# Float32 value product on two halves of the array, and a stick-breaking product moved to GpSimd

## The chip, the cores and the metric

The kernel runs on one core of a Trainium2 chip. Its engines are TensorE (PE, with weight loads as PEld), VectorE (DVE), ScalarE (ACT), GpSimd (POOL) and SyncE (SP, which issues the DMAs). The metric is the device time of one execution in microseconds, lower is better.

## The reference

One layer of a hybrid encoder block on 2048 tokens of 1024 channels: RMSNorm, one input projection, a Mamba-2 SSD branch, a stick-breaking attention branch with 16 heads of 64 channels, a gated merge, an output projection, RMSNorm and the residual. The change lies in the attention branch:

```
logits = einsum('bqhd,bkhd->bhqk', q[:, q0:kend], k[:, :kend]) * scale
mask = ki < qi
log_fail = where(mask, log_sigmoid(-logits), 0)
between = cumsum(log_fail, reverse) - log_fail
w = where(mask, exp(log_sigmoid(logits) + between), 0)
out = einsum('bhqk,bkhd->bqhd', w, v[:, :kend])
```

The kernel takes the sum of logarithms as a running product: t = sigmoid(-logits) is multiplied from the newest key to the oldest, and w = sigmoid(logits) times the running product of the keys behind.

## The kernel before

Everything that is projected from the input goes through `product`: weights and activations are each split in a high and a low fp32r part, and three fp32r products of 512 columns stand for one float32 product. The projections of v go to DRAM (`vst`) with both parts beside each other, 64 + 64 columns a head; k and q lie in `kst` and `qst`, split in the same way. After the SSD stage (whose state output `yp` is made by float32 products with 64 columns of weights) follows the attention loop over `steps`: a step is (head h, 512 queries qs, 512 keys kc), 160 in all, keys from the diagonal block (kc = qs) backward. Of the ten steps of a head four are diagonal and six are full.

A step works on four query blocks of 128 (i) and four key blocks of 128 (kb). `attn_qk(s + 1, i)` makes the logits `lg` of query block i in the next step by two fp32r products, two sigmoids on ScalarE (t in tile `tc`, w in tile `sw`), on diagonal steps two affine selects on GpSimd (L847, L849), the running product as a scan on VectorE (L852), and the product of w and the running product on VectorE (L853). GpSimd copies the scan's last column (`cy`, L856) as the start of the next step's scan, and sets one column of `tc` to 1. `attn_tr(s, kb)` transposes the weights of key block kb on TensorE: one transposition for each query block, all into one tile `wtp`; `attn_tr(s, 0)` reads all four `sw` tiles of the step. ScalarE and VectorE split the result in `wh` and `wl` (L870, L872), and `attn_av` multiplies both with v into `po`.

All products and transpositions are chained on TensorE in the order in which the code writes them (`chain`). Into the gaps `fill(i)` puts products of projections that are needed later: 3264 of them over the first 150 steps, spread over the places of a step by the weights FW, and with them the evictions, stores and weight preparation that belong to them. The last head's ten steps are filled with the first products of the next stage (`fill_y`), prepared by `first_y`, which also puts sums on GpSimd (L695).

Of the kernel before, what the change touches and what calls it, by code (L numbers as in the profile page):

```python
# [23 lines left out]
HD = 64  # L24
EPS = 1e-6
WARM = 24
FW = (0.8, 0.9, 1.0, 1.0, 1.1, 1.2)

COL_Z = 0
COL_X = 1024  # L30
# [18 lines left out]
def hybrid_kernel(ctx, tc, x, norm_pre, w_in, b_gate, conv_w, conv_b, dt_bias, a_log, d_skip,  # L49
# [57 lines left out]

    kst = [drp.tile([P, L], F32, name=f"kst{h}") for h in range(HEADS)]
    qst = [drp.tile([P, L], F32, name=f"qst{h}") for h in range(HEADS)]
    vst = [drp.tile([L, 4, P], F32, name=f"vst{i}") for i in range(HEADS // 4)]  # L110
    csd = drp.tile([HEADS, L], F32, name="csd")
    ytd = [drp.tile([D, TB], F32, name=f"ytd{t}") for t in range(NTB)]
    otd = [drp.tile([D, TB], F32, name=f"otd{t}") for t in range(NTB)]
# [272 lines left out]
    with tc.tile_pool(name="va", bufs=2) as va, tc.tile_pool(name="vp", bufs=2, space=PSUM) as vp:  # L386
# [16 lines left out]
        def unit_v(i, c, wv):  # L403
            c0, cw = vch[i]
            vh, vl = wv
            off = cw - VW
            tb, o = c // CPB, (c % CPB) * P
            ps = vp.tile([P, TB], F32, name="vps", tag="vps", bufs=3)
            for k in range(KT):
                xh, xl = hh[tb][:, k, o:o + P], hl[tb][:, k, o:o + P]  # L410
                matmul(ps[:, :cw], xh, vh[k], start=(k == 0), stop=False)
                yield
                matmul(ps[:, :cw], xh, vl[k], start=False, stop=False)
                yield
                matmul(ps[:, :cw], xl, vh[k], start=False, stop=(k == KT - 1))
                yield
            if off:
                nc.vector.tensor_copy(kn[:, c, :], ps[:, :16])
            v = va.tile([P, 4, 2, HD], F32R, name="vt", tag="vt", bufs=3)
            src = ps[:, off:cw].rearrange("p (h d) -> p h d", d=HD)  # L420
            nc.scalar.copy(v[:, :, 0, :], src)
            nc.vector.tensor_sub(v[:, :, 1, :], src, v[:, :, 0, :].bitcast(F32))
            nc.sync.dma_start(vst[i][c * P:(c + 1) * P], v.bitcast(F32).rearrange("p h s d -> p h (s d)"))

        def last_k():
            knf = kn.rearrange("p c d -> p (c d)")
# [352 lines left out]

    steps = [(h, qs, kc) for h in range(HEADS) for qs in reversed(range(NTB)) for kc in reversed(range(qs + 1))]  # L780
    last_head = min(i for i, s in enumerate(steps) if s[0] == HEADS - 1)
    fills = {"gen": fill_h(), "left": n_main, "pos": 6 * last_head, "acc": 0.0, "late": False}

    def tick():
        clock[0] += 1
# [3 lines left out]
    def fill(i):  # L789
        f = fills  # L790
        if f["pos"] <= 0:
            for _ in f["gen"]:
                tick()
            if f["late"]:
                return
            f.update(gen=fill_y(box_y), left=8 * 24, pos=6 * (len(steps) - last_head) - 3, acc=0.0, late=True)
        f["acc"] += f["left"] / f["pos"] * FW[i]
        f["pos"] -= 1
        while f["acc"] >= 1.0:
            f["acc"] -= 1.0  # L800
            f["left"] -= 1
            if next(f["gen"], 0) == 0:
                f["left"] = 0
                break
            tick()
# [3 lines left out]
    def attn_load(s):  # L809
# [11 lines left out]
        if (h, kc) not in kts:  # L821
            k = ab.tile([P, TB], F32R, name="kt", tag="kt", bufs=4)
            nc.sync.dma_start(k.bitcast(F32), kst[h][:, kc * TB:(kc + 1) * TB])
            v = ab.tile([P, CPB, P], F32R, name="vt", tag="vt", bufs=4)
            nc.sync.dma_start(v.bitcast(F32), vst[h // 4][kc * TB:(kc + 1) * TB, h % 4, :].rearrange(
                "(c p) d -> p c d", p=P))
            kts[h, kc], vts[h, kc] = k, v

    def attn_qk(s, i):
# [20 lines left out]
                                    pattern=[[-1, P]], channel_multiplier=1)  # L850
        tr = t[:, W::-1]
        nc.vector.tensor_tensor_scan(tr, tr, tr, 1.0 if diag else carry[h, qs, i], ALU.mult, ALU.min)  # L852
        nc.vector.tensor_mul(w[:, :W], w[:, :W], t[:, 1:W + 1])  # L853
        if kc > 0:
            c = ab.tile([P, 1], F32, name="cy", tag="cy", bufs=8)
            nc.gpsimd.tensor_copy(c, t[:, 0:1])  # L856
# [5 lines left out]
    def attn_tr(s, kb):  # L862
        h, qs, kc = steps[s]
        q0 = kb if kc == qs else 0
        lo = q0 * P
        tp = ap.tile([P, TB], F32, name="wtp", tag="wtp", bufs=3)
        for i in range(q0, CPB):
            transpose(tp[:, i * P:(i + 1) * P], ws[s, i][:, kb * P:(kb + 1) * P], ident)
        wh = ab.tile([P, TB], F32R, name="wh", tag="wh", bufs=3)
        nc.scalar.copy(wh[:, lo:], tp[:, lo:])  # L870
        wl = ab.tile([P, TB], F32R, name="wl", tag="wl", bufs=3)
        nc.vector.tensor_sub(wl[:, lo:], tp[:, lo:], wh[:, lo:].bitcast(F32))  # L872
        wts[s, kb] = lo, wh, wl

    def attn_av(s, kb):
        h, qs, kc = steps[s]
        lo, wh, wl = wts.pop((s, kb))
        if (h, qs) not in pos:
            pos[h, qs] = ap.tile([P, TB], F32, name="po", tag="po", bufs=1)
        po, v = pos[h, qs], vts[h, kc]  # L880
        first = kc == qs and kb == 0
        final = kc == 0 and kb == CPB - 1
        matmul(po[:, lo:], v[:, kb, :], wh[:, lo:], start=first, stop=False, skip_group_check=True)
        matmul(po[:, lo:], v[:, kb, :], wl[:, lo:], start=False, stop=final, skip_group_check=True)
        if final:
            e0 = (h % 2) * HD
            mine, other = slice(e0, e0 + HD), slice(HD - e0, P - e0)
            z = ab.tile([P, TB], F32, name="zl", tag="zl", bufs=1)
# [15 lines left out]
    for s in range(len(steps)):  # L904
        attn_load(s + 2)
        for i in range(CPB):
            attn_tr(s, i)
            attn_qk(s + 1, i)
            if i >= 2:
                attn_av(s, i - 2)  # L910
            fill(i)
        for i in range(2, CPB):
            attn_av(s, i)
            fill(i + 2)
    for _ in fills["gen"]:
        pass
    close_ap()
# [150 lines left out]
```

## Time and profile before

| | |
|---|---|
| median of 3 runs (lowest, highest) | 3164.92 us (3163.69, 3165.49) |
| span of the profiled execution | 3163.6 us |
| TensorE products, busy | 3024.1 us (96%) |
| TensorE weight loads, busy | 2496.9 us (79%) |
| VectorE, busy | 2457.2 us (78%) |
| ScalarE, busy | 1585.7 us (50%) |
| GpSimd, busy | 477.9 us (15%) |
| mean granted TensorE clock | 0.993 |

The span is that of one profiled execution, from its first to its last instruction; durations in the text come from it. A record of a product on TensorE is longer than the time until the next one starts, since products overlap in the array; so TensorE's busy share says little of how full it is, and the starts are what counts. The attention loop takes the time from 936 us to about 2663 us.

### The profile page before, as it was taken

How to read it: one execution, taken by the hardware profiler on the slowest of the kernel's cores; microseconds unless marked ns; L12 is line 12 of the kernel's file. 1: busy time of each engine (PE TensorE's matmuls, PEld its weight loads, DVE VectorE, ACT ScalarE, POOL GpSimd, SP SyncE). 2: the span in 40 equal slices, each digit the busy share in tenths (PEclk: the TensorE clock that was granted, in tenths of full speed). 3: DMA queues.
4: the chain of work that ended last, by engine and by line, in shares of the span. 5: the costliest groups of instructions: out<-in, count | busy, mean ns of one | idle time of the engine just before them, and what ended most of it. 6: DMA issues, size and time to landing. Idle time of an engine off the chain costs nothing.

```text
span 3163.6 us, 48155 instructions
## 1 busy us (share of the span) xinstructions
PE 3024.1 (96%) x16169; PEld 2496.9 (79%) x16169; DVE 2457.2 (78%) x4357; ACT 1585.7 (50%) x3102; POOL 477.9 (15%) x1626
## 2 busy tenths in 40 slices
PE   8999999999999999999999999999999989999998
PEld 6899888787877777777777777777777767888887
DVE  7321688768869989989899999989998899756553
ACT  6211345434446666566565666566665656333321
POOL 0000011100111212122212121222111231101000
PEclk9999999999999999999999999999999999999999
DMA  5532022212243334224323333334233334555452
GB/s 165 148 122 93 24 71 80 68 40 67 72 128 89 90 89 110 80 81 113 93 70 103 94 97 91 87 94 114 69 89 90 111 117 144 176 148 167 133 167 70
DMA packets 298816, 320.63 MB, mean 101 GB/s; under 512 B 23148, under 2 KB 187848, under 8 KB 298568
## 3 DMA queue, kind: packets, MB, share of 16 engines
q1 hardware_dynamic: 298416, 317.51, 34.6%
q8 instruction: 128, 2.10, 0.3%
q14 instruction: 120, 0.98, 0.1%
q10 hardware_dynamic: 152, 0.05, 0.0%
HBM read 216.67 MB, written 100.79 MB: 100 GB/s over the span
## 4 chain that ended last, share of the span: by engine, by line
PE 53%; DVE 33%; issue 5%; DMA 4%; ACT 4%; POOL 1%; SPq 0%; DVEq 0%; POOLq 0%; ACTq 0%
PE proj L74 30%; DVE tc L852 13%; PE po L74 8%; DVE sw L853 7%; PE vps L74 6%; DVE wl L872 5%; PE wtp L77 4%; PE lg L74 3%; DMA csb<-csd 2%; ACT sw L845 1%; ACT wh L870 1%; PE yp L74 1%; DVE acc L474 1%; DVE o L893 1%; DVE o L892 1%
## 5 line engine op out<-in xcount | busy, mean ns | idle before, releaser
L74 PE MATMUL proj<-hh,whi 128*128 128x512 f32 x1920 | 762.0, 397 | 0.1
L74 PE MATMUL proj<-hh,wlo 128*128 128x512 f32 x1920 | 761.7, 397 | 0.0
L74 PE MATMUL proj<-hl,whi 128*128 128x512 f32 x1920 | 760.4, 396 | 1.3 <-DVE hl L286 1.1
L870 ACT CAST wh<-wtp 128x512 fp32r<-128x512 f32 (+3 forms) x640 | 337.1, 527 | 390.2 <-PE wtp L77 386.6
L852 DVE TENSOR_TENSOR_SCAN tc<-tc,cy 128x513 f32<-128x513 f32 x384 | 490.9, 1278 | 0.3 <-ACT tc L843 0.3
L872 DVE TENSOR_TENSOR wl<-wtp,wh 128x512 fp32r<-128x512 f32 (+3 forms) x640 | 383.0, 599 | 81.5 <-ACT wh L870 80.3
L77 PE MATMUL wtp<-ident,sw 128*128 128x128 f32 x2176 | 369.9, 277 | 72.2 <-DVE sw L853 70.1
L853 DVE TENSOR_TENSOR sw<-sw,tc 128x512 f32<-128x512 f32 (+3 forms) x640 | 394.2, 616 | 50.5 <-POOL sw L849 13.5
L77 PEld LDWEIGHTS wtp<-ident,sw 128*128 128x128 f32 x2176 | 280.7, 141 | 181.0 <-DVE sw L853 99.1
L74 PEld LDWEIGHTS proj<-hl,whi 128*128 128x128 f32 x1920 | 362.6, 189 | 72.6 <-DVE hl L286 2.5
L74 PEld LDWEIGHTS proj<-hh,wlo 128*128 128x128 f32 x1920 | 362.6, 189 | 70.7 <-issue 0.3
L74 PEld LDWEIGHTS proj<-hh,whi 128*128 128x128 f32 x1920 | 362.7, 189 | 70.1 <-ACT hh L285 0.5
L845 ACT ACTIVATE sw<-lg 128x512 f32<-128x512 f32 (+3 forms) x640 | 346.1, 541 | 49.8 <-PE wtp L77 49.6
L843 ACT ACTIVATE tc<-lg 128x512 f32<-128x512 f32 (+3 forms) x640 | 349.1, 545 | 18.7 <-PE lg L74 13.1
L132 ACT CAST whi<-wraw 128x512 fp32r<-128x512 f32 x248 | 154.3, 624 | 280.5 <-PE proj L74 178.9
L74 PE MATMUL lg<-kt,qa 128*128 128x512 f32 (+3 forms) x640 | 285.1, 445 | 0.0
L74 PE MATMUL po<-wl,vt 128*128 128x512 f32 (+3 forms) x640 | 242.6, 379 | 29.0 <-DVE wl L872 28.2
L852 DVE TENSOR_TENSOR_SCAN tc<-tc 128x129 f32<-128x129 f32 (+3 forms) x256 | 218.1, 852 | 26.3 <-POOL tc L847 25.2
L74 PE MATMUL lg<-kt,qb 128*128 128x512 f32 (+3 forms) x640 | 234.6, 367 | 0.0
L74 PE MATMUL po<-wh,vt 128*128 128x512 f32 (+3 forms) x640 | 232.4, 363 | 0.0
L134 DVE TENSOR_TENSOR wlo<-wraw,whi 128x512 fp32r<-128x512 f32 x246 | 173.4, 706 | 73.3 <-ACT whi L132 70.5
L856 POOL COPY cy<-tc 128x1 f32<-128x1 f32 x384 | 133.6, 348 | 448.7 <-DVE tc L852 448.7
(202 smaller groups left out, 4887.8 us busy)
## 6 DMA issues: line engine op xcount, KB each, us to landing
wraw<-in_w_in SPq DMA_DIRECT2D x120, 256.0 KB, 3.0
vst<-vt SPq DMA_DIRECT2D x64, 256.0 KB, 2.0
csb<-csd SPq DMA_DIRECT2D x64, 256.0 KB, 4.4
qa<-qst SPq DMA_DIRECT2D x64, 256.0 KB, 3.5
qb<-qst SPq DMA_DIRECT2D x128, 128.0 KB, 3.8
kt<-kst SPq DMA_DIRECT2D x64, 256.0 KB, 3.2
vt<-vst SPq DMA_DIRECT2D x64, 256.0 KB, 3.0
gtd<-zb SPq DMA_DIRECT2D x64, 256.0 KB, 2.1
```

What stands on the lines that cost most here:

```text
L74: chain(nc.tensor.matmul(*a, **k))
L77: chain(nc.tensor.transpose(*a))
L132: nc.scalar.copy(h, raw)
L134: (eng or nc.vector).tensor_tensor(l, raw, h.bitcast(F32), op=ALU.subtract)
L474: nc.vector.scalar_tensor_tensor(acc, xp[:, i:i + TB], pv[:, col:col + 1], acc, op0=ALU.mult, op1=ALU.add)
L843: nc.scalar.activation(t[:, :W], lg[:, :W], AF.Sigmoid, scale=-0.125)
L845: nc.scalar.activation(w[:, :W], lg[:, :W], AF.Sigmoid, scale=0.125)
L852: nc.vector.tensor_tensor_scan(tr, tr, tr, 1.0 if diag else carry[h, qs, i], ALU.mult, ALU.min)
L853: nc.vector.tensor_mul(w[:, :W], w[:, :W], t[:, 1:W + 1])
L856: nc.gpsimd.tensor_copy(c, t[:, 0:1])
L870: nc.scalar.copy(wh[:, lo:], tp[:, lo:])
L872: nc.vector.tensor_sub(wl[:, lo:], tp[:, lo:], wh[:, lo:].bitcast(F32))
```

## The change

The value product becomes one float32 product for each key block: v is stored and loaded as it is, without a split, the transposed weights are copied once (`wt`), and the 64 columns of v stand as weights on the lower or the upper half of the array, by the parity of the key block. Each half sums its own two key blocks in its half of `po`; the two halves are added at the end as before. On diagonal steps key block 1 is widened to all 512 columns, with zeros. All four value products of step s - 1 are now issued in step s, after its second query block. The fill has five places a step in place of six. The product of stick weight and running product moves from VectorE to GpSimd.

```diff
--- before.py
+++ after.py
@@ -24,7 +24,7 @@
 HD = 64
 EPS = 1e-6
 WARM = 24
-FW = (0.8, 0.9, 1.0, 1.0, 1.1, 1.2)
+FW = (1.0, 1.0, 1.2, 1.2, 0.6)
 
 COL_Z = 0
 COL_X = 1024
@@ -107,7 +107,7 @@
 
     kst = [drp.tile([P, L], F32, name=f"kst{h}") for h in range(HEADS)]
     qst = [drp.tile([P, L], F32, name=f"qst{h}") for h in range(HEADS)]
-    vst = [drp.tile([L, 4, P], F32, name=f"vst{i}") for i in range(HEADS // 4)]
+    vst = [drp.tile([P, 4, NCH, HD], F32, name=f"vst{i}") for i in range(HEADS // 4)]
     csd = drp.tile([HEADS, L], F32, name="csd")
     ytd = [drp.tile([D, TB], F32, name=f"ytd{t}") for t in range(NTB)]
     otd = [drp.tile([D, TB], F32, name=f"otd{t}") for t in range(NTB)]
@@ -416,11 +416,9 @@
                 yield
             if off:
                 nc.vector.tensor_copy(kn[:, c, :], ps[:, :16])
-            v = va.tile([P, 4, 2, HD], F32R, name="vt", tag="vt", bufs=3)
-            src = ps[:, off:cw].rearrange("p (h d) -> p h d", d=HD)
-            nc.scalar.copy(v[:, :, 0, :], src)
-            nc.vector.tensor_sub(v[:, :, 1, :], src, v[:, :, 0, :].bitcast(F32))
-            nc.sync.dma_start(vst[i][c * P:(c + 1) * P], v.bitcast(F32).rearrange("p h s d -> p h (s d)"))
+            v = va.tile([P, 4, HD], F32, name="vt", tag="vt", bufs=3)
+            nc.scalar.copy(v, ps[:, off:cw].rearrange("p (h d) -> p h d", d=HD))
+            nc.sync.dma_start(vst[i][:, :, c, :], v)
 
         def last_k():
             knf = kn.rearrange("p c d -> p (c d)")
@@ -779,7 +777,7 @@
 
     steps = [(h, qs, kc) for h in range(HEADS) for qs in reversed(range(NTB)) for kc in reversed(range(qs + 1))]
     last_head = min(i for i, s in enumerate(steps) if s[0] == HEADS - 1)
-    fills = {"gen": fill_h(), "left": n_main, "pos": 6 * last_head, "acc": 0.0, "late": False}
+    fills = {"gen": fill_h(), "left": n_main, "pos": len(FW) * last_head, "acc": 0.0, "late": False}
 
     def tick():
         clock[0] += 1
@@ -793,7 +791,7 @@
                 tick()
             if f["late"]:
                 return
-            f.update(gen=fill_y(box_y), left=8 * 24, pos=6 * (len(steps) - last_head) - 3, acc=0.0, late=True)
+            f.update(gen=fill_y(box_y), left=8 * 24, pos=len(FW) * (len(steps) - last_head) - 3, acc=0.0, late=True)
         f["acc"] += f["left"] / f["pos"] * FW[i]
         f["pos"] -= 1
         while f["acc"] >= 1.0:
@@ -821,9 +819,8 @@
         if (h, kc) not in kts:
             k = ab.tile([P, TB], F32R, name="kt", tag="kt", bufs=4)
             nc.sync.dma_start(k.bitcast(F32), kst[h][:, kc * TB:(kc + 1) * TB])
-            v = ab.tile([P, CPB, P], F32R, name="vt", tag="vt", bufs=4)
-            nc.sync.dma_start(v.bitcast(F32), vst[h // 4][kc * TB:(kc + 1) * TB, h % 4, :].rearrange(
-                "(c p) d -> p c d", p=P))
+            v = ab.tile([P, CPB, HD], F32, name="vt", tag="vt", bufs=4)
+            nc.sync.dma_start(v, vst[h // 4][:, h % 4, kc * CPB:(kc + 1) * CPB, :])
             kts[h, kc], vts[h, kc] = k, v
 
     def attn_qk(s, i):
@@ -850,7 +847,7 @@
                                     pattern=[[-1, P]], channel_multiplier=1)
         tr = t[:, W::-1]
         nc.vector.tensor_tensor_scan(tr, tr, tr, 1.0 if diag else carry[h, qs, i], ALU.mult, ALU.min)
-        nc.vector.tensor_mul(w[:, :W], w[:, :W], t[:, 1:W + 1])
+        nc.gpsimd.tensor_tensor(w[:, :W], w[:, :W], t[:, 1:W + 1], op=ALU.mult)
         if kc > 0:
             c = ab.tile([P, 1], F32, name="cy", tag="cy", bufs=8)
             nc.gpsimd.tensor_copy(c, t[:, 0:1])
@@ -866,23 +863,24 @@
         tp = ap.tile([P, TB], F32, name="wtp", tag="wtp", bufs=3)
         for i in range(q0, CPB):
             transpose(tp[:, i * P:(i + 1) * P], ws[s, i][:, kb * P:(kb + 1) * P], ident)
-        wh = ab.tile([P, TB], F32R, name="wh", tag="wh", bufs=3)
-        nc.scalar.copy(wh[:, lo:], tp[:, lo:])
-        wl = ab.tile([P, TB], F32R, name="wl", tag="wl", bufs=3)
-        nc.vector.tensor_sub(wl[:, lo:], tp[:, lo:], wh[:, lo:].bitcast(F32))
-        wts[s, kb] = lo, wh, wl
-
-    def attn_av(s, kb):
+        wt = ab.tile([P, TB], F32, name="wt", tag="wt", bufs=6)
+        nc.scalar.copy(wt[:, lo:], tp[:, lo:])
+        if lo == P:
+            nc.gpsimd.memset(wt[:, :lo], 0.0)
+            lo = 0
+        wts[s, kb] = lo, wt
+
+    def attn_av(s):
         h, qs, kc = steps[s]
-        lo, wh, wl = wts.pop((s, kb))
         if (h, qs) not in pos:
             pos[h, qs] = ap.tile([P, TB], F32, name="po", tag="po", bufs=1)
         po, v = pos[h, qs], vts[h, kc]
-        first = kc == qs and kb == 0
-        final = kc == 0 and kb == CPB - 1
-        matmul(po[:, lo:], v[:, kb, :], wh[:, lo:], start=first, stop=False, skip_group_check=True)
-        matmul(po[:, lo:], v[:, kb, :], wl[:, lo:], start=False, stop=final, skip_group_check=True)
-        if final:
+        for kb in range(CPB):
+            lo, wt = wts.pop((s, kb))
+            e = (kb % 2) * HD
+            matmul(po[e:e + HD, lo:], v[:, kb, :], wt[:, lo:], start=(kc == qs and kb < 2),
+                   stop=(kc == 0 and kb >= 2), skip_group_check=True)
+        if kc == 0:
             e0 = (h % 2) * HD
             mine, other = slice(e0, e0 + HD), slice(HD - e0, P - e0)
             z = ab.tile([P, TB], F32, name="zl", tag="zl", bufs=1)
@@ -906,12 +904,11 @@
         for i in range(CPB):
             attn_tr(s, i)
             attn_qk(s + 1, i)
-            if i >= 2:
-                attn_av(s, i - 2)
             fill(i)
-        for i in range(2, CPB):
-            attn_av(s, i)
-            fill(i + 2)
+            if i == 1 and s > 0:
+                attn_av(s - 1)
+                fill(CPB)
+    attn_av(len(steps) - 1)
     for _ in fills["gen"]:
         pass
     close_ap()
```

TensorE's order where one step of the first heads ends and the next begins (`proj` is the fill, `wtp` the transpositions, of which the group at the end is `attn_tr` of key block 0 of the next step). Before, two pairs of `po` with four `proj` between them stand behind the step's last `lg`, and then these rows:

```order
L74 MATMUL proj<-hh_195,wlo 128x512
L74 MATMUL proj<-hh_195,whi 128x512
L74 MATMUL proj<-hl_199,whi 128x512
L74 MATMUL proj<-hh_195,wlo 128x512
L74 MATMUL po<-wh,vt 128x512
L74 MATMUL po<-wl,vt 128x512
L74 MATMUL proj<-hh_195,whi 128x512
L74 MATMUL proj<-hl_199,whi 128x512
L74 MATMUL proj<-hh_195,wlo 128x512
L74 MATMUL proj<-hh_195,whi 128x512
L77 MATMUL wtp<-ident,sw 128x128 x4
```

After, with `attn_tr` of key block 3 and the `lg` of query block 3 at the start:

```order
L77 MATMUL wtp<-ident,sw 128x128 x4
L74 MATMUL lg<-kt,qa 128x512
L74 MATMUL lg<-kt,qb 128x512
L74 MATMUL proj<-hh_194,whi 128x512
L74 MATMUL proj<-hl_198,whi 128x512
L74 MATMUL proj<-hh_194,wlo 128x512
L74 MATMUL proj<-hh_195,whi 128x512
L74 MATMUL proj<-hl_199,whi 128x512
L77 MATMUL wtp<-ident,sw 128x128 x4
```

Between the last `lg` and the transpositions of the next step stood three pairs of `po` and twelve `proj`; now five `proj` stand there.

GpSimd's order on a diagonal step, query blocks 1 to 3 before (`tc` and `sw` are the tiles of the two sigmoids):

```order
L847 AFFINE_SELECT tc<-tc 128x128
L849 AFFINE_SELECT sw<-sw 128x128
L856 COPY cy<-tc 128x1
L842 MEMSET tc 128x1
L847 AFFINE_SELECT tc<-tc 128x128
L856 COPY cy<-tc 128x1
L849 AFFINE_SELECT sw<-sw 128x128
L842 MEMSET tc 128x1
L847 AFFINE_SELECT tc<-tc 128x128
L849 AFFINE_SELECT sw<-sw 128x128
L856 COPY cy<-tc 128x1
```

And after, query blocks 0 to 2 and the start of block 3:

```order
L844 AFFINE_SELECT tc<-tc 128x128
L846 AFFINE_SELECT sw<-sw 128x128
L850 TENSOR_TENSOR sw<-sw,tc 128x128
L853 COPY cy<-tc 128x1
L839 MEMSET tc 128x1
L844 AFFINE_SELECT tc<-tc 128x128
L846 AFFINE_SELECT sw<-sw 128x128
L850 TENSOR_TENSOR sw<-sw,tc 128x256
L853 COPY cy<-tc 128x1
L839 MEMSET tc 128x1
L844 AFFINE_SELECT tc<-tc 128x128
```

The product `sw<-sw,tc` is new in this queue; the affine select of the next query block stands behind it and behind the copy `cy`.

## Rows read from the trace of the kernel before

**Rows 1.** The page's chain that ended last, shares by engine.
```profile
PE 53%; DVE 33%; issue 5%; DMA 4%; ACT 4%; POOL 1%; SPq 0%; DVEq 0%; POOLq 0%; ACTq 0%
```

**Rows 2.** Timeline of TensorE: start us, us, operation [idle before <-releaser].
```profile
935.61 0.49 PE L77 MATMUL wtp<-ident,sw 128*128 128x128 f32 x3
...
2427.88 0.49 PE L77 MATMUL wtp<-ident,sw 128*128 128x128 f32 x3
...
2561.17 0.53 PE L77 MATMUL wtp<-ident,sw 128*128 128x128 f32 x3
2563.82 0.33 PE L77 MATMUL wtp<-ident,sw 128*128 128x128 f32 x1 [2.11 <-DVE sw L853]
```

**Rows 3.** Timeline of TensorE in a full step.
```profile
1606.20 0.60 PE L77 MATMUL wtp<-ident,sw 128*128 128x128 f32 x4
...
1607.10 0.40 PE L74 MATMUL po<-wh,vt 128*128 128x512 f32 x1
...
1607.57 0.39 PE L74 MATMUL proj<-hh,whi 128*128 128x512 f32 x1
...
1608.50 0.40 PE L74 MATMUL po<-wh,vt 128*128 128x512 f32 x1
```

**Rows 4.** Groups by line: busy us, mean ns of one | idle before.
```profile
L852 DVE TENSOR_TENSOR_SCAN tc<-tc,cy 128x513 f32<-128x513 f32 x384 | 490.9, 1278 | 0.3 <-ACT tc L843 0.3
L853 DVE TENSOR_TENSOR sw<-sw,tc 128x512 f32<-128x512 f32 (+3 forms) x640 | 394.2, 616 | 50.5 <-POOL sw L849 13.5 <-ACT tc L843 0.5
L872 DVE TENSOR_TENSOR wl<-wtp,wh 128x512 fp32r<-128x512 f32 (+3 forms) x640 | 383.0, 599 | 81.5 <-ACT wh L870 80.3
...
L976 POOL TENSOR_TENSOR scr<-scr 128x512 f32<-128x512 f32 x16 | 20.7, 1292 | 226.3 <-DVE scr L975 203.8 <-DVE scr L99 22.5
```

**Rows 5.** Timeline of TensorE in the SSD stage.
```profile
805.16 0.39 PE L74 MATMUL proj<-hl,whi 128*128 128x512 f32 x1
805.48 0.44 PE L74 MATMUL yp<-dl,xd 128*64 128x128 f32 x4
...
807.06 0.39 PE L74 MATMUL yp<-csb,S 128*64 128x128 f32 x4
...
812.90 1.05 PE L74 MATMUL stp<-xe,bn 128*128 128x128 f32 x8
```

**Rows 6.** Timeline of all engines, last head.
```profile
2511.61 1.28 DVE L852 TENSOR_TENSOR_SCAN tc<-tc,cy 128x513 f32<-128x513 f32 x1
...
2511.92 2.02 POOL L695 TENSOR_TENSOR mp<-mp 128x512 f32<-128x512 f32 x1
...
2512.99 1.50 DVE L853 TENSOR_TENSOR sw<-sw,tc 128x512 f32<-128x512 f32 x1
...
2514.62 2.09 DVE L852 TENSOR_TENSOR_SCAN tc<-tc,cy 128x513 f32<-128x513 f32 x1
```

**Rows 7.** Timeline of all engines, two steps.
```profile
1603.20 0.40 PE L74 MATMUL proj<-hh,wlo 128*128 128x512 f32 x1
...
1603.46 0.60 ACT L843 ACTIVATE tc<-lg 128x512 f32<-128x512 f32 x1
...
1613.12 0.28 ACT L843 ACTIVATE tc<-lg 128x128 f32<-128x128 f32 x1
...
1613.47 0.29 POOL L847 TENSOR_SCALAR_AFFINE_SELECT tc<-tc 128x128 f32<-128x128 f32 x1 [1.10 <-ACT tc L843]
...
1613.86 0.42 DVE L852 TENSOR_TENSOR_SCAN tc<-tc 128x129 f32<-128x129 f32 x1
...
1614.35 0.19 POOL L856 COPY cy<-tc 128x1 f32<-128x1 f32 x1 [0.34 <-DVE tc L852]
```

**Rows 8.** Windows: length, busy us (x) of PE, PEld, DVE, ACT, POOL, then PEclk, DMA.
```profile
936.10:938.40 2.30, 0.04 (x2) 0.04 (x1) 2.07 (x3) 0.76 (x2) 0.52 (x3) 1.00 0.68 220
938.40:945.00 6.60, 6.60 (x33) 5.44 (x34) 6.16 (x9) 5.58 (x12) 0.67 (x5) 1.00 0.17 44
2561.70:2563.80 2.10, 0.01 (x1) 0.00 (x0) 2.10 (x4) 0.61 (x1) 0.19 (x1) 1.00 0.00 0
2565.00:2568.20 3.20, 2.76 (x9) 2.26 (x9) 3.13 (x4) 1.44 (x4) 0.69 (x2) 0.50 0.54 160
```

## The prediction

> **What bounds the kernel now.** I read the chain of work that ended last first: TensorE holds 53% of it and VectorE 33% [rows 1]. Neither alone sets the end, so I took the longest stage apart, the attention loop. In TensorE's timeline the first transposition of step 0 starts at 935.61 us and that of step 140 at 2427.88 us: 140 steps, 10.66 us each [rows 2]. A step's own work on TensorE adds up from the starts in [rows 3]: four transpositions and the two lg products of one query block take 0.90 us, two po products 0.47 us, four proj products 0.93 us, so 0.232 us for a product and (0.90 - 0.46) / 4 = 0.11 us for a transposition. The fill gives 3264 proj products to 150 steps, 21.8 a step, or 5.05 us. A full step (a key block ahead of the diagonal) is then 4 x 0.90 + 4 x 0.47 + 5.05 = 10.53 us. Four of a head's ten steps are diagonal, with six transpositions and 1536 of 4096 columns of lg and of po fewer each (0.66 + 0.70 + 0.70 us): the mean is 9.71 us. TensorE thus waits only 0.95 us a step. Where it waits can be seen: three transpositions run, and the fourth, which needs the newest query block's stick weights, waits for the product that makes them, once for 2.11 us [rows 2]. VectorE's load for each full query block is scan 1.28, product 0.62 and remainder 0.60 us in the means [rows 4], so 10 us in four of them: both engines set the pace by turns.
>
> **What the change removes.** 640 remainders (383.0 us) and 640 products (394.2 us) leave VectorE [rows 4], and the remainders of v in the projection stage, where TensorE sets the time and nothing comes back. All that VectorE's load costs now lies inside the 0.95 us a step that TensorE waits: at most 160 x 0.95 = 152 us can be won.
>
> **The value product.** For each key block two fp32r products of 512 columns become one float32 product with 64 columns of weights, on alternating halves of the array. The state output of the SSD stage, yp, has this form with 128 columns: two heads on two halves. Each of its float32 products leaves two records, and 32 records in eight groups of four start from 805.48 us on, 0.226 us from group to group [rows 5]; the last group ends 1.97 us after the first start. On the full width eight records of stp take 1.05 us [rows 5], so 32 would take over 3.5. Pairs do run side by side. With 512 columns a pair is 4 x 0.226 = 0.90 us and two pairs 1.81 us, where 1.88 us stood. Entering the half-array form costs 0.09 us (0.32 us from the last proj to the first yp [rows 5], in place of 0.23); I take as much for leaving it, an estimate, and so 2.0 us a full step. The bounds are nothing, and pairs that do not overlap (a rival). On a diagonal step it is 0.45 us less. TensorE's own work rises by 0.1 to 0.3 us a step.
>
> **The product on GpSimd.** A GpSimd operation on two 512-wide tiles in SBUF takes 1.29 us, VectorE's product 0.62 in the mean [rows 4]. 640 x 1.29 = 826 us at most, in a stage of 1700 us: GpSimd is not full. But the two engines get in each other's way. A GpSimd sum that starts at 2511.92, during a scan, takes 2.02 us; VectorE's next product takes 1.50 us, and its next scan 2.09 in place of 1.28 us [rows 6]. That scan starts 0.13 us after the product's end and is 0.81 us late, so a GpSimd operation of this size keeps a scan out for 0.94 us. For a full step that is 4 x (1.28 + 0.94) = 8.9 us of exclusive time, less than the step: no bound by throughput. The Trainium skill (SBUF — State Buffer, Who interferes with whom) has such a pair exclude each other for the whole instruction. By that a scan would be kept out for 1.29 us, and the path below would be 0.35 us a step longer, 56 us in all; the trace's rows show the shorter time.
>
> **The wait that is added** is the largest term. TensorE keeps the program's order. Before, three pairs of po (1.41 us) and 3.3 weights of fill (3.3 x 3264 / 900 = 12 proj, 2.78 us) stand between the lg products of the next step's query block 3 and the transpositions that need its stick weights: 4.2 us of cover. After, all four po products stand earlier, behind block 1, and only fill(3) is left: 1.2 x 3264 / 750 = 5.2 proj, 1.21 us. With three transpositions that can run, 0.33 us, the cover is 1.54 us.
> What has to be done in that time is a chain through four engines, in which a freer VectorE shortens nothing. From the end of lg's stream (1603.20, where the next product starts) to the start of the sigmoid 0.26 us, the sigmoid 0.60 [rows 7]; a hop from engine to engine 0.07 to 0.10 us [rows 7]; scan 1.28; GpSimd product 1.29 [rows 4]. Sum 0.26 + 0.60 + 0.10 + 1.28 + 0.07 + 1.29 + 0.07 = 3.67 us. Block 2 runs 2.11 us ahead of block 3 (0.90 us and fill(2), 1.21 us); counted from the end of block 3's lg its scan ends at 0.13 us, and its product, a hop later, keeps block 3's scan out until 1.14, which is 0.18 us after that could start at 0.96: 3.85 us. If the next step is diagonal, an affine select (0.29 us, a hop of 0.07) comes between sigmoid and scan and queues on GpSimd behind block 2's product and its copy (0.19 us) [rows 7]: an estimate of 0.58 more, 4.43 us. Behind the waiting transposition stands all of TensorE's queue.
> A step is then TensorE's work from the end of the wait to the last lg, plus the chain. The work: 3.60 - 0.33 for transpositions and lg, 3.8 x 4.35 x 0.232 = 3.84 for fill, 2.0 for po, 9.11 us; in four steps of ten each 0.66 less (a diagonal step), 0.70 less (diagonal step next) and 0.45 less (diagonal step before, in po); mean 8.39. The chain: 0.6 x 3.85 + 0.4 x 4.43 = 4.08. A step is 12.47 us, 1.81 more than 10.66; times 160 that is 290 us.
>
> **The clock.** TensorE would then lie idle for 2.2 to 2.8 us in every step. After the wait of 2.1 us at 2561.7 us the granted clock is 0.50, the lower level (1.2 GHz), from 2565.0 for at least 3.2 us; after one of 2.3 us at 936.1 it stays at 1.00 [rows 8]. Seven idle stretches of 1.9 us and more stand behind the first 60 us, two of them close together; five falls go with them, and only that at 936.1 has none. I take a fall in three steps of four: 120 falls, each 3.2 us at half rate while TensorE has work, 1.6 us lost: 192 us. The bounds are no fall, and one in every step (256 us).
>
> **Edits at nothing.** The stores to vst shrink from 256 to 128 KB, in pieces of 256 bytes, and the loads shrink too. What hides them is a prefetch of two steps; DMA has 4% of the chain [rows 1]. The zero fill of wt comes once a diagonal step, far ahead of its use. Without this cover it would be a few us.
>
> **The sum.** The profiled execution's span is 3163.6 us and the median of the three runs 1.3 us more. 3163.6 + 290 + 192 + 1.3 = 3647 us.
>
> **Rivals.** (a) The wait comes and the clock holds: 3455 us. For it speaks 936.1 us; against it the five falls. (b) The pairs do not run side by side. A pair then costs 0.90 us more, which is 1.8 us in a full and 1.35 us in a diagonal step, 260 us in all: 3715 us without the falls and 3907 with them. Against it: yp. (c) The other side: VectorE's queue and not the chain is what TensorE waits for, and block 3 is ready in time. The step falls to its own work, 8.39 + 0.33 + 1.21 = 9.93 us, and the time to 3164.9 - 160 x 0.73 = 3048 us. This needs a chain of at most 1.54 us; up to 10.66 - 8.39 = 2.27 us the change would still win. Against it: scan and GpSimd product alone are 2.57 us [rows 4]. (d) The chain is up to 1.2 us shorter than I make it, by a GpSimd product that ends sooner and a scan that starts before its sigmoid's record ends, and the idle stretches become too short for falls: 3263 to 3430 us. For it: a scan is kept out for only 0.94 us.
>
> **How the numbers follow.** Forecast 0.50, (a) 0.24, (b) 0.09, (c) 0.06, (d) 0.11. The range leaves out (c), (d) and the upper half of (b): 3430 to 3800 us. A measurement of this kernel tells about 0.2% from no change. Faster is (c), 0.06; within 0.2% I give 0.02, out of (d); slower 0.92.
>
> **What the new profile would show.** Right: transpositions that wait 2.2 us or more for GpSimd's product sw, some 160 times; steps of 12 to 14 us; a granted clock clearly below 1 through the attention loop; two po products in 0.9 us; VectorE some 800 us less busy. Wrong: transpositions that wait less than 1 us; GpSimd products far below 1.2 us; po products one after the other; scans of 2 us throughout, by which the shared access to SBUF, and not the chain, would be the bound.

## The result, and the profile after

The changed kernel takes 3704.18 us, median of 4 runs (3701.15 to 3709.5), beside 3165.03 us before in the same session: a ratio of 1.171, 95% interval [1.169, 1.172]. It is 539 us slower; 3647 us was forecast, with 3430 to 3800 as the range.

From the page of the changed kernel: the span, the granted clock in 40 slices, the chain's shares by engine, and three groups by line (busy us, mean ns of one | idle before, releaser).
```profile
span 3707.8 us, 47088 instructions
...
PEclk9999999999989889889889988899889988999999
...
PE 65%; DVE 15%; POOL 9%; ACT 5%; issue 3%; DMA 3%; POOLq 0%; SPq 0%; DVEq 0%; ACTq 0%
...
L850 POOL TENSOR_TENSOR sw<-sw,tc 128x512 f32<-128x512 f32 (+3 forms) x640 | 630.0, 984 | 884.6 <-DVE tc L849 722.1
L849 DVE TENSOR_TENSOR_SCAN tc<-tc,cy 128x513 f32<-128x513 f32 x384 | 538.3, 1402 | 589.9 <-ACT tc L840 571.7
...
L77 PE MATMUL wtp<-ident,sw 128*128 128x128 f32 x2176 | 446.3, 305 | 404.9 <-POOL sw L850 393.3
```
The last of these groups before the change:
```profile
L77 PE MATMUL wtp<-ident,sw 128*128 128x128 f32 x2176 | 369.9, 277 | 72.2 <-DVE sw L853 70.1
```
The shares of the chain differ from [rows 1]: VectorE's falls from 33% to 15%, and GpSimd's rises from 1% to 9%. The scans are the same work as in [rows 4], but take 1402 ns in place of 1278. The transpositions waited 70 us for the product before, and now 393 us. In 11 slices of the attention loop the granted clock is below 0.9 (the digit 8); before, no slice was.

Timeline of all engines, the newest query block at the end of a step (start us, us, operation [idle before <-releaser]).
```profile
1718.08 0.39 PE L74 MATMUL lg<-kt,qb 128*128 128x512 f32 x1
...
1718.31 0.40 PE L74 MATMUL proj<-hl,whi 128*128 128x512 f32 x1
...
1718.62 1.09 POOL L850 TENSOR_TENSOR sw<-sw,tc 128x512 f32<-128x512 f32 x1 [2.61 <-DVE tc L849]
1718.67 0.62 ACT L840 ACTIVATE tc<-lg 128x512 f32<-128x512 f32 x1
...
1719.39 1.41 DVE L849 TENSOR_TENSOR_SCAN tc<-tc,cy 128x513 f32<-128x513 f32 x1 [0.92 <-ACT tc L840]
1719.47 0.62 PE L77 MATMUL wtp<-ident,sw 128*128 128x128 f32 x3
...
1720.97 1.09 POOL L850 TENSOR_TENSOR sw<-sw,tc 128x512 f32<-128x512 f32 x1 [1.10 <-DVE tc L849]
...
1722.11 0.33 PE L77 MATMUL wtp<-ident,sw 128*128 128x128 f32 x1 [2.02 <-POOL sw L850]
...
1722.54 0.74 PE L74 MATMUL proj<-hh,whi 128*128 128x512 f32 x1
1723.08 0.63 PE L74 MATMUL proj<-hl,whi 128*128 128x512 f32 x1
```
This is the chain of the forecast: logits, sigmoid, scan, product, and then the fourth transposition, which has waited 2.02 us. From the end of lg's stream (1718.31) to that transposition it took 3.80 us. All the cover that TensorE had was five proj and three transpositions. Behind the wait the records of the proj products are 0.74 and 0.63 us long, in place of 0.40.

Windows of TensorE's clock: the attention stage, the cover ahead of that wait, and the stretch behind it (length, busy us (x) of PE, PEld, DVE, ACT, POOL, then PEclk, DMA share, GB/s).
```profile
934.40:3203.00 2268.60, 1862.22 (x8209) 1298.60 (x8207) 968.06 (x968) 1076.59 (x2223) 970.26 (x2240) 0.90 0.24 68
...
1722.54:1726.00 3.46, 3.46 (x13) 2.88 (x14) 0.49 (x1) 1.00 (x4) 1.18 (x5) 0.53 0.00 0
1718.31:1719.47 1.16, 1.16 (x6) 0.90 (x5) 0.24 (x2) 1.16 (x4) 0.85 (x1) 1.00 0.11 32
```
TensorE runs at full clock up to the wait and near the lower level (0.53) behind it. Over the whole stage the clock is 0.90 in the mean. In the trace's clock records the stage has 114 stretches at 0.50, 474 us in all, and TensorE works in 436 of them; before, it had 7 with 27 us, and worked in 25.

A step now takes (2910.61 - 934.42) / 140 = 14.12 us, by the first transpositions of steps 0 and 140, as in [rows 2]; before it took 10.66. From its first transposition to its last the attention stage is 2268.7 us long and was 1727.1 (935.6 to 2662.7): 542 of the 544 us by which the span of the profiled execution grew. All else together moved by less than 3 us.

### The profile page after: what moved, and what is told of

Same layout as the page of the kernel before. It is cut to its first block, busy times and chain, and to the rows that moved or that the text cites. A ratio compares the mean times of both kernels' runs of the same rounds, so it can differ in the third digit from the quotient of the medians.

```text
span 3707.8 us, 47088 instructions
## 1 busy us (share of the span) xinstructions
PE 3267.1 (88%) x16169; PEld 2492.6 (67%) x16169; DVE 1823.1 (49%) x3013; ACT 1603.8 (43%) x3102; POOL 1069.9 (29%) x2330
## 4 chain that ended last, share of the span: by engine, by line
PE 65%; DVE 15%; POOL 9%; ACT 5%; issue 3%; DMA 3%; POOLq 0%; SPq 0%; DVEq 0%; ACTq 0%
PE proj L74 34%; PE po L74 11%; DVE tc L849 9%; POOL sw L850 6%; PE wtp L77 6%; PE lg L74 6%; PE vps L74 5%; ACT tc L840 2%; DMA csb<-csd 2%; ACT wt L867 1%; POOL tc L844 1%; PE yp L74 1%; DVE acc L472 1%; POOL sw L846 1%; DVE S L538 1%
## 5 line engine op out<-in xcount | busy, mean ns | idle before, releaser
L850 POOL TENSOR_TENSOR sw<-sw,tc 128x512 f32<-128x512 f32 (+3 forms) x640 | 630.0, 984 | 884.6 <-DVE tc L849 722.1
L849 DVE TENSOR_TENSOR_SCAN tc<-tc,cy 128x513 f32<-128x513 f32 x384 | 538.3, 1402 | 589.9 <-ACT tc L840 571.7
L74 PE MATMUL proj<-hh,whi 128*128 128x512 f32 x1920 | 808.5, 421 | 0.1
L74 PE MATMUL proj<-hl,whi 128*128 128x512 f32 x1920 | 806.6, 420 | 1.2 <-DVE hl L286 0.9
L77 PE MATMUL wtp<-ident,sw 128*128 128x128 f32 x2176 | 446.3, 305 | 404.9 <-POOL sw L850 393.3
L867 ACT COPY wt<-wtp 128x512 f32<-128x512 f32 (+3 forms) x640 | 334.4, 523 | 929.6 <-PE wtp L77 925.4
L504 POOL TENSOR_TENSOR xe<-xd,dec 128x512 f32<-128x512 f32 x32 | 49.8, 1556 | 831.1 <-DVE xd L502 831.1
L74 PE MATMUL po<-wt,vt 128*64 128x512 f32 (+2 forms) x1280 | 284.2, 555 | 0.0
L74 PEld LDWEIGHTS po<-wt,vt 128*64 128x64 f32 x1280 | 78.5, 137 | 153.1 <-issue 151.1
L844 POOL TENSOR_SCALAR_AFFINE_SELECT tc<-tc 128x128 f32<-128x128 f32 x256 | 77.2, 302 | 288.0 <-ACT tc L840 285.4
```

Source lines behind the costliest of these rows:

```text
L74: chain(nc.tensor.matmul(*a, **k))
L77: chain(nc.tensor.transpose(*a))
L504: nc.gpsimd.tensor_tensor(heads(xe), heads(xd), tok(dec), op=ALU.mult)
L844: nc.gpsimd.affine_select(out=t[:, W - P:W], in_=t[:, W - P:W], compare_op=ALU.is_gt, fill=1.0, base=0, pattern=[[-1, P]], channel_multipl ...
L850: nc.gpsimd.tensor_tensor(w[:, :W], w[:, :W], t[:, 1:W + 1], op=ALU.mult)
L867: nc.scalar.copy(wt[:, lo:], tp[:, lo:])
```

## The experiments

Each ratio is to the kernel before, run on the same chip. "Step" is the mean of the first 140. "Chain" is the time from the start of the second lg product of the newest query block to the transposition that waits for it; "low clock" is the time at 0.50 in the stage.

**1. Something for TensorE to do in the wait.** Seven products that nobody reads go into the tile of the first transpositions, ahead of them, in each step.
```diff
+        if kb == 0 and s > 0:
+            for _ in range(7):
+                matmul(tp, qts[h, qs][0][:, :P], kts[h, kc], start=True, stop=True)
         for i in range(q0, CPB):
             transpose(tp...
```


> Seven extra fp32r products of 512 columns (1.6 us), whose result nothing uses, stand ahead of the first transpositions of each step, inside the wait. Wait-and-clock theory: they fit into the idle 2.0 to 2.7 us, leave 0.4 to 1.1 us idle, the granted clock stays at 1.00, and the 237 us that the 474 us at half rate cost come back: 3704 - 237 = about 3470 us (3440 to 3530). Rival, the clock is no cost of its own (the falls lie in time that is lost anyway): no change or slower, 3690 to 3960 us.

3520.31 us, ratio 1.112 [1.1105, 1.1138]: 184 us come back by work that is of no use. The window of the middle of the stage:
```profile
936.00:2100.00 1164.00, 1074.53 (x5272) 769.63 (x5273) 554.53 (x522) 595.48 (x1244) 556.62 (x1267) 1.00 0.25 72
```
The clock is 1.00 there; 31 us at the lower level are left in the stage. The chain has the same length as in the changed kernel (4.36 us on full steps, 4.33 there). So the clock is a cost of its own, which goes with the idle stretches and not with the amount of useful work. Half of the time at the lower level in which TensorE works would be 205 us, (436 - 25) / 2; 184 came back. The added products don't run past the wait: behind them TensorE is still idle for 0.34 us or more in every step. But at full clock steps of the same kind are 0.02 to 0.13 us longer than in the changed kernel, some 11 us in all; the rest stays open.

**2. The order of the value products on the halves.**
```diff
-        for kb in range(CPB):
+        for kb in (0, 2, 1, 3):
```


> The four value products of a step are issued in the order of key blocks 0, 2, 1, 3, so that neighbours stand on the same half of the array. If halves overlap only between neighbours: seven passes of 0.43 us in place of four, 1.2 us more in a full and 0.9 us in a diagonal step, 175 us in all: 3880 us (3820 to 3950). If TensorE pairs them whatever the order, or pairs never overlapped: 3704 us.

3704.36 us, ratio 1.171 [1.1691, 1.173]: no difference. In the timeline the four value products of a full step take as long as in the changed kernel. There:
```profile
1726.65 0.39 PE L74 MATMUL proj<-hh,wlo 128*128 128x512 f32 x1
1726.97 1.94 PE L74 MATMUL po<-wt,vt 128*64 128x512 f32 x8
1728.84 0.50 PE L74 MATMUL proj<-hh,whi 128*128 128x512 f32 x1
```
With products of one half next to each other in the program, in this run:
```profile
1723.75 1.95 PE L74 MATMUL po<-wt,vt 128*64 128x512 f32 x8
```
By itself this leaves open whether the products overlap in either order or in neither; experiment 3 tells.

**3. All four value products on one half.** The sum of the two halves is left out with it, as one half holds everything.
```diff
-            e = (kb % 2) * HD
+            e = HD - (h % 2) * HD
...
-            nc.vector.tensor_add(o[mine], o[mine], po[mine])
```


> The changed kernel with all four value products of a step on the same half of the array, so that no two can run side by side; the sum of the two halves is left out, since one half holds all. If side by side is what halves their price: 8 passes of 0.43 us in place of 4 on a full step (1.7 us more), 1.0 us more on a diagonal one, 230 us in all: 3930 us (3870 to 3990). Rival, products on the two halves never overlapped: 3704 us.

3875.88 us, ratio 1.224 [1.2211, 1.2274]: 172 us more. The same four products:
```profile
1721.19 3.65 PE L74 MATMUL po<-wt,vt 128*64 128x512 f32 x8
```
They take 3.65 in place of 1.94 us, so in the changed kernel the pairs do run side by side, and by experiment 2 whatever their order. A step takes 15.13 us, 1.01 more, which is less than these 1.71 us: diagonal steps have smaller products, and TensorE works at the lower level for 308 us in place of 436, which gives (436 - 308) / 2 = 64 us back.

**4. The product back on VectorE.**
```diff
-        nc.gpsimd.tensor_tensor(w[:, :W], w[:, :W], t[:, 1:W + 1], op=ALU.mult)
+        nc.vector.tensor_mul(w[:, :W], w[:, :W], t[:, 1:W + 1])
```


> The product of stick weight and running product goes back to VectorE, all else as changed. Wait-and-clock theory: the chain loses 1.09 - 0.68 us and about 0.2 us of keeping the scan out, 0.6 us in all; the wait stays at 1.4 to 2.0 us a step, so 100 us come back from the wait and some 100 from rarer falls: 3500 us (3430 to 3600). Rival, the product on GpSimd is the whole loss: 3150 to 3250 us.

3482.06 us, ratio 1.100 [1.0986, 1.1019], step 12.64 us. The chain is 3.69 us on full steps in place of 4.33, the low clock 212 us in place of 474. That is 222 of the 539 us; 317 stay without any product on GpSimd. Those are lost by the value products and their place (7 tells these two apart).

**5. The fill later in the step.** The weights of the fill move towards the place ahead of the wait.
```diff
-FW = (1.0, 1.0, 1.2, 1.2, 0.6)
+FW = (0.6, 0.6, 0.8, 2.6, 0.4)
```


> Only the weights of the fill are changed, so that 2.6 of 5 parts stand between the newest logits and the transpositions, in place of 1.2. Wait-and-clock theory: cover grows by 1.41 us, the wait shrinks to 0.6 to 1.3 us, few falls: 3704 - 225 - 200 = 3280 us (3220 to 3360). Rival, GpSimd and scan bound the step by their throughput: 3650 to 3710 us.

3401.6 us, ratio 1.075 [1.0729, 1.0761]: 303 us better, but 42 us above the range. The step is 12.12 us. The low clock went down to 116 us; what was missed is that the chain got longer, 4.84 us on full and 5.19 on diagonal steps. On full steps the product started 0.58 us behind the scan, not 0.22: with the blocks closer together it had to wait in GpSimd's queue. In 33 of the 90 full steps it starts over 0.3 us behind the scan, right behind the operation ahead of it on GpSimd; in the changed kernel the gap is that long in 4.

**6. The value products at the end of the step.** They again stand ahead of the wait, as all of the cover did before the change.
```diff
-            if i == 1 and s > 0:
-                attn_av(s - 1)
-                fill(CPB)
-    attn_av(len(steps) - 1)
+        attn_av(s)
+        fill(CPB)
```


> The four value products of a step and the last fill are issued at the end of the same step, between the newest logits and the transpositions that need them. Wait-and-clock theory: cover 1.21 + 2.0 + 0.61 + 0.33 = 4.15 us against a chain of 3.8 to 4.4 us, so waits under 0.5 us, no falls, a step of 10.0 to 10.6 us: 3050 to 3170 us. Rival, GpSimd's product and its exclusive use of SBUF with the scan bound the step: over 3400 us. Rival, the float32 value product is dear: over 3500 us.

3234.57 us, ratio 1.023 [1.0209, 1.0243]: 470 of 539 us come back by the place of the value products and the last fill alone, at a clock of 0.99. But it isn't faster than before, and it lies 65 us above the range that I expected, short of both rivals. The groups by line:
```profile
L850 POOL TENSOR_TENSOR sw<-sw,tc 128x512 f32<-128x512 f32 (+3 forms) x640 | 701.7, 1096 | 532.8 <-DVE tc L849 398.5 <-ACT wt L867 75.7 <-ACT tc L840 30.6
L849 DVE TENSOR_TENSOR_SCAN tc<-tc,cy 128x513 f32<-128x513 f32 x384 | 598.6, 1570 | 300.8 <-ACT tc L840 292.9 <-POOL tc L839 2.8 <-POOL sw L850 1.8
L77 PE MATMUL wtp<-ident,sw 128*128 128x128 f32 x2176 | 385.0, 279 | 138.2 <-POOL sw L850 134.6 <-DMA qb<-qst 1.8 <-DMA gtd<-zb 0.2
...
L853 POOL COPY cy<-tc 128x1 f32<-128x1 f32 x384 | 182.6, 476 | 32.8 <-DVE tc L849 32.8
```
The scans take 1570 ns and the copies of one column 476, in the changed kernel 1402 and 293. Still 135 us of waits for GpSimd are left. Something other than the missing cover costs here, and the next experiments go after it.

**7. The same order with the product on VectorE.** The edits of 4 and 6 together.


> Value products and last fill at the end of their step, and the product on VectorE. Wait-and-clock theory: cover 4.15 us against a chain of 3.1 to 3.6 us, no wait but for VectorE's own queue of about 7.6 us a full step: 3040 to 3130 us. Rival, the float32 value product is dear for TensorE: 3300 us and more.

3101.11 us, ratio 0.981 [0.9793, 0.9822], step 10.30 us. Between this and experiment 6 lies only the engine of the product: 133 us. And the rest of the change, under cover, is 1.9% faster than the kernel before; how much of that comes from the float32 value product on TensorE and how much from the remainders that VectorE is spared was not separated.
```profile
L849 DVE TENSOR_TENSOR_SCAN tc<-tc,cy 128x513 f32<-128x513 f32 x384 | 494.0, 1286 | 86.9 <-ACT tc L840 85.2 <-POOL tc L839 0.2
...
L77 PE MATMUL wtp<-ident,sw 128*128 128x128 f32 x2176 | 357.9, 275 | 35.6 <-DVE sw L850 35.2 <-DMA qb<-qst 0.3
...
L853 POOL COPY cy<-tc 128x1 f32<-128x1 f32 x384 | 74.7, 194 | 439.4 <-DVE tc L849 439.4
```

**8. The kernel before, with only the product on GpSimd.** One line of the kernel before, the reverse of 4.


> The kernel before with one edit, the product of stick weight and running product on GpSimd. Wait-and-clock theory: cover of 4.2 us against a chain of 3.8 to 4.4 us, VectorE 2.4 us a step freer: waits under 0.7 us, 3080 to 3230 us. Rival, the product on GpSimd is the loss by itself (slow, and in the scan's way): 3400 us and more.

3258.18 us, ratio 1.031 [1.0288, 1.0331]: 96 us more than before (3162.44 us on that chip), though the wait has all the cover of before. That is above the first range and far below the rival's.
```profile
L852 DVE TENSOR_TENSOR_SCAN tc<-tc,cy 128x513 f32<-128x513 f32 x384 | 619.6, 1614 | 5.3 <-ACT tc L843 4.5 <-POOL sw L853 0.3 <-POOL cy L856 0.3
L77 PE MATMUL wtp<-ident,sw 128*128 128x128 f32 x2176 | 387.8, 280 | 151.5 <-POOL sw L853 149.6 <-DMA qb<-qst 1.2 <-DMA wraw<-in_w_in 0.7
```
The scans take 1614 ns in the mean, where they took 1278, and the waits for the product are 150 us, where they were 70. So the product on GpSimd is a loss in both programs, without any help from the value product.

**9. The copy of the carry on VectorE**, on the kernel of 6.
```diff
-            nc.gpsimd.tensor_copy(c, t[:, 0:1])
+            nc.vector.tensor_copy(c, t[:, 0:1])
```


> The version with the value products at the end of their step (3235 us), with the copy of the scan's last column on VectorE in place of GpSimd. In its trace 93 of 384 copies take over 0.9 us, since a scan keeps them out, and the next product queues behind them. If that queue on GpSimd is what the covered order still waits for: 3150 to 3200 us. Rival, the product's own 1.1 us and its exclusion with the scan: 3220 to 3245 us.

3213.67 us, ratio 1.015 [1.0139, 1.0169]: 21 us better, between the two ranges and nearer to the rival's. The 384 copies take 0.15 us each on VectorE, but the 512-wide products on GpSimd now take 1.34 us in the mean, not 1.28. So I take it that part of the wait for a scan's end has moved from the copy to the product behind it.

**10. More cover**, on the kernel of 6: the fill moves to the end of the step.
```diff
-FW = (1.0, 1.0, 1.2, 1.2, 0.6)
+FW = (0.7, 0.8, 0.9, 1.3, 1.3)
```


> The version with the value products at the end of their step and the product on GpSimd (3235 us), with 0.8 us more fill between the newest logits and the transpositions. If what it still waits for is the length of the chain (5.2 us against 4.15 us of cover): 3235 - 0.8 x 160 = about 3110 us (3100 to 3170). Rival, scan and GpSimd product, which exclude each other, set the pace by their sum: 3215 to 3240 us.

3203.09 us, ratio 1.012 [1.0106, 1.014]: 31 us better. That is nearer to the rival's range than to the other, and in neither. A chain of fixed length could have been covered; this one grows with the cover (5.84 us on full steps, 5.19 in 6). What it looks like, on GpSimd:
```profile
1596.95 1.10 POOL L850 TENSOR_TENSOR sw<-sw,tc 128x512 f32<-128x512 f32 x1 [2.16 <-ACT tc L840]
1597.99 1.12 POOL L853 COPY cy<-tc 128x1 f32<-128x1 f32 x1
...
1599.30 1.89 POOL L850 TENSOR_TENSOR sw<-sw,tc 128x512 f32<-128x512 f32 x1
1601.14 1.12 POOL L853 COPY cy<-tc 128x1 f32<-128x1 f32 x1
...
1602.44 1.10 POOL L850 TENSOR_TENSOR sw<-sw,tc 128x512 f32<-128x512 f32 x1
1603.48 0.18 POOL L853 COPY cy<-tc 128x1 f32<-128x1 f32 x1
...
1603.84 1.09 POOL L850 TENSOR_TENSOR sw<-sw,tc 128x512 f32<-128x512 f32 x1
...
1604.99 0.33 PE L77 MATMUL wtp<-ident,sw 128*128 128x128 f32 x1 [1.07 <-POOL sw L850]
```
and on VectorE:
```profile
1596.95 5.33 DVE L849 TENSOR_TENSOR_SCAN tc<-tc,cy 128x513 f32<-128x513 f32 x3 [0.17 <-ACT tc L840]
```
Three scans stand back to back from 1596.95 to 1602.28, 1.78 us each. In that time GpSimd gets through two products, of 1.10 and 1.89 us, and two copies, of 1.12 us each where a free one takes 0.18. When the last scan ends, two products stand one behind the other, and the transposition waits for the second: 1604.99 - 1602.28 = 2.7 us after the last scan.

**11. The same fill with the product on VectorE**, the edit of 10 on the kernel of 7.


> The version with the value products at the end of their step and the product on VectorE (3101 us), with weights of fill that put 0.8 us more between the newest logits and the transpositions. If TensorE there still waits for the chain (4.5 us against 4.15 us of cover): 3060 to 3090 us. Rival, what is left is TensorE's own work and VectorE's queue: 3095 to 3110 us.

3089.57 us, ratio 0.976 [0.9745, 0.9774]: the fastest version, at the upper end of the first range. The step is 10.25 us.

**12. Only the newest block's product on VectorE**, on the kernel of 10.
```diff
+        if i == CPB - 1:
+            nc.vector.tensor_mul(w[:, :W], w[:, :W], t[:, 1:W + 1])
+        else:
-        nc.gpsimd.tensor_tensor(w[:, :W], w[:, :W], t[:, 1:W + 1], op=ALU.mult)
+            nc.gpsimd.tensor_tensor(w[:, :W], w[:, :W], t[:, 1:W + 1], op=ALU.mult)
```


> This is the kernel with the value products at the end of the step and more fill behind them (3203 us with every product on GpSimd, 3090 with every product on VectorE), with the product of the newest query block alone back on VectorE; three of four stay on GpSimd. The 113 us between those two are either paid by the last product of the chain (it is longer on GpSimd, and it stands behind two older products and their copies in GpSimd's queue), or by the exclusion itself, that is by scans and products that keep each other out wherever they stand. First theory: the queue behind the last scan is gone, so 3090 to 3115 us, steps of 10.25 to 10.4 us and less than 0.3 us from the end of the newest block's scan to its product. Second theory: the product on VectorE has to wait for GpSimd's products and the scans are still late, so 3135 to 3175 us, with a gap of 0.5 us or more. I expect 3120, nearer the first: most of what was lost stood in GpSimd's queue behind the last scan.

3134.69 us, ratio 0.991 [0.9892, 0.9925], step 10.49 us: the time lies at the edge of the second theory's range, while the gap behind the scan, which falls from 1.27 to 0.27 us on full steps, is that of the first. Both are at work. Of the 113 us between 10 and 11, 68 come back with a quarter of the products, those behind which TensorE waits. 45 us stay with the other three quarters.
```profile
L849 DVE TENSOR_TENSOR_SCAN tc<-tc,cy 128x513 f32<-128x513 f32 x384 | 588.6, 1557 | 139.4 <-ACT tc L840 134.4 <-POOL sw L853 1.0 <-issue 0.2
L853 POOL TENSOR_TENSOR sw<-sw,tc 128x512 f32<-128x512 f32 x288 | 442.0, 1535 | 328.8 <-DVE tc L849 181.4 <-PE wtp L77 56.5 <-ACT wt L870 37.4
...
L851 DVE TENSOR_TENSOR sw<-sw,tc 128x512 f32<-128x512 f32 x160 | 149.5, 934 | 19.7 <-DVE tc L849 0.5 <-POOL cy L856 0.5
```
The newest products take 0.93 us on VectorE (0.70 in 11), the GpSimd products 1.54 us, the scans still 1.56.

## Why the prediction was right, and where it was off

**What bounds, and what could be won.** Right: less work on VectorE won nothing here. The groups removed hold 804 us (777 in the loop, 27 in the projection of v); the page's busy time of VectorE falls by 634 (2457.2 to 1823.1). The scans are 54 us longer in sum (763 and 709 us). Most of the rest is how the page counts: it takes time in which two records overlap once, and such overlap falls from 232 to 122 us.

**The value product.** Right in mechanism and size: from the last proj ahead of the four to the first behind them it takes 1728.84 - 1726.65 = 2.19 us, less the 0.23 of that proj 1.96; 2.0 was forecast. Experiment 3 excludes rival (b) for the changed kernel, and confirms its price about: 172 us plus the 64 that the clock gave back is 236, where 260 stood.

**The wait.** Right in mechanism, a little too low in size. The clock's part is 205 us by the paragraph on the clock below, so 544 - 205 = 339 us are left for the wait, forecast 290. Experiments 5 and 6 confirm the cause: cover alone, by fill or by place, gives back 303 and 470 us, the clock's part included. The term that was too small is the chain. Counted from the end of lg's stream it takes 4.10 us on full and 4.63 on diagonal steps (4.33 and 4.86 less the 0.23 of the second lg product), forecast 3.85 and 4.43; the mean of 4.31 is 0.23 us above the forecast's 4.08, which is 37 of these 49 us in 160 steps.
The parts on full steps, from 90 of them and counted from the same point: the scan could start at 1.11, forecast 0.96, and ends at 2.73, forecast 2.42. It takes 1.62 us in place of 1.28, so it was kept out for 0.34 us, where the forecast had 0.18. The gap from scan to product is 0.22, forecast 0.07; the product 1.10, forecast 1.29 from a line that does a sum. The forecast had block 2 too early: its scan ends at 0.32, forecast 0.13, and its product, behind a gap of 0.20, ends at 1.67. The affine select adds 0.53, forecast 0.58.
Of the signs named ahead, the wait of 2.2 us or more holds in 73 of 160 steps; 157 steps wait 1.9 us or more. The mean wait is 2.05 us on full and 2.73 us on diagonal steps.
In the rows above block 2's product ends at 1719.71 and the scan, 0.13 us longer than alone, at 1720.80: it really began at about 1719.52, 0.19 us before the product's record ends. Over all 76 full steps where the scan was kept out, this is 0.20 us. The forecast's 0.94 us came from the same thing, though not from the sum that [rows 6] show, which ends at 2513.94; it is the next one that stands beside the late scan of 2514.62:
```profile
2513.91 1.72 POOL L695 TENSOR_TENSOR scr<-scr 128x512 f32<-128x512 f32 x1
```
It ends at 2515.63, and the scan, by its length alone, began at 2515.43. The Trainium skill (SBUF — State Buffer, SBUF: two separate sides) has a VectorE instruction with two inputs in SBUF and a GpSimd instruction that reads SBUF exclude each other for the whole instruction. For GpSimd behind a scan the rows agree: the 35 copies of over 0.9 us in the changed kernel all end 0.02 us before the scan does. For a scan behind GpSimd's product the rows show 0.20 us less than its whole record; since a profile gives GpSimd's spans only roughly, this doesn't decide against that section.

**The clock.** Right in mechanism, a little too low in size: 114 falls were shown where 120 were forecast, but each gives 436 / 114 = 3.8 us in which TensorE works at half rate, in place of 3.2. Half of 436 us is 218; the seven falls before, with 25 us of work, had cost 13, so the change adds 205 us, forecast 192. The steps agree: the 144 of 147 steps of experiment 1 that ran at full clock took 12.88 us in the mean, and the changed kernel's few steps at full clock are about 0.07 us shorter than those of the same kind there. By that its step at full clock is 12.81 us, and the 14.12 us hold 1.31 for the clock, 210 us in 160 steps. The forecast took each fall's length from one stretch of [rows 8], which it named as a least length ("at least 3.2 us"). The 13 us of the clock and the 49 of the wait make 62; the profiled execution, at 3709.5 us, is 5 us above the median, which leaves the miss of 57. Both terms were too low, so neither made up for the other. Rival (a), the clock that holds, is excluded; experiment 1 shows 184 us of it directly.

**Exclusive access.** Here the prediction left something out, though it cost the number little. "No bound by throughput" was worked out as 4 x (1.28 + 0.94) = 8.9 us in a step. In the changed kernel, with steps of 14.12 us, it holds: the idle TensorE spreads the blocks out, and the gap behind the scan is 0.22 us. Where the cover is there, the blocks come close together, and the sum has to count more: GpSimd takes its operations one behind the other, a copy of 0.18 us that meets a scan holds it for 1.12 us, and the products stand behind. Experiments 6 against 7 (133 us), 8 against before (96 us) and 10 against 11 (113 us) show the price of the product on GpSimd. Of the 113, experiment 12 puts 68 on the products that TensorE waits for and 45 on the others; of the 133, experiment 9 puts 21 on the copies. How the 68 us divide between the longer duration and the queue was not separated.

**The other rivals.** (c) needed a chain of at most 1.54 us, and it was 4.1. Its 3048 us are what TensorE's own work would give, and with order, cover and the product on VectorE the kernel comes to 3090. (d) saw the shorter product rightly (1.10 us), but the later scan took that back.

**Edits at nothing.** Right: of 405 us of idle time ahead of the transpositions, 7 are put down to loads of q and k, 393 to GpSimd's product.

## What to carry to other kernels

Before work is moved on an engine that runs in order, count what stands between a result's first step and its reader, before and after: here 4.2 us of cover became 1.5 us, against a chain of 4 us, and moving the same products, with some fill, back to that place was worth 470 us. Idle stretches of TensorE have a second price in the granted clock, which here added 205 us to the wait's own 339. And an operation given to GpSimd beside VectorE's scans is not paid by its own duration: sum what each keeps the other out, small copies in the same queue included, in the densest order that the kernel should reach. Here that price was 96 to 133 us wherever the wait had cover.

## What was not expected of the hardware

Products on different halves of the array did not keep the program's order among each other. In experiment 2, on a diagonal step, the program has products of 512 and 256 columns for one half and then 512 and 128 for the other; in the single records the two of 512 start 13 ns apart and, 0.91 us later, those of 256 and 128, 12 ns apart. It is so in 63 of the 64 diagonal steps. The second product of the program's order is overtaken by the third. In the changed kernel, with the halves alternating, it is 7 ns, and the time is the same. The Trainium skill (TensorE: Matmul & The Clock Gate, Step-by-step: what each phase is for) says that products stay in program order; for these two halves the records show otherwise.

A GpSimd copy of one column takes 0.18 us, and about 1.12 us when it meets a scan: in experiment 6 over 0.9 us in 93 of 384 cases, each of which ends 0.02 us before a scan does.
